# Expert rows gathered as two half rows from two tables instead of as whole rows from one, beside weight streaming with six raw buffers

## Chip, cores and metric

One core of a Trainium2 chip. The metric is device time in microseconds of one execution of the whole layer. The kernel before takes 2120.93 us, the median of 3 runs (2119.68 to 2122.23).

## What is computed

One encoder layer over 256 tokens of width 2048, all in float32. Two mixers and a cross attention come first. The last part, and the one that the change touches, is a feed-forward layer of 16384 single-neuron experts: for each token, 8 heads choose their 16 best experts each, and

```
u = u_tab[eb]
act = jax.nn.gelu(jnp.einsum('td,tkd->tk', xb, u))
out = jnp.einsum('tk,tkd->td', gb * act, v_tab[eb])
```

with `eb` the 128 chosen experts of a token and `gb` their softmax gates. `u_tab` and `v_tab` have 16384 rows of 2048 numbers (8 KB). The result is added to the tokens and normalized.

## The kernel before

The experts are split into two groups on the host. Three quarters (96 of 128 groups of 128 experts) are handled densely: all tokens times all of these experts, as matrix products on TensorE (PE), with the gates of experts that a token did not choose at zero. The other quarter (4096 experts, tables `Us` and `Vs`) is handled sparsely: for each token the rows of its chosen experts are gathered from memory.

Dense side. The products come in 12 chunks of 1024 experts. A weight tile of 128x1024 numbers, 512 KB, is loaded by SP's DMA queue into a raw buffer (`raw`), ACT rounds it to a high part (`hi`, line 1079), VectorE (DVE) subtracts to get the low part (`lo`, line 1085), and PE multiplies with both (lines 128 and 131 for `U`; 939 to 941 for `V`). The function `run` (line 1066) walks a list of such steps by hand-written lead times: `load(t + 8)`, `high(t + 3)`, `low(t + 2)`, then the products of step t. There are six raw buffers there (lines 1068 and 1069: four of the pool and two more), and the load into a buffer waits for DVE's `low` that read it last. A step may also be a load of gate values (`gd`), which DVE multiplies into the activations (line 1033). The list holds first steps of `V` and `U` chunks in turn, then steps of `V` alone.

Sparse side. `chosen` (line 1156) makes a list of tasks, each for one slot of all 128 tokens of a half: a `dot` (line 1139) on DVE multiplies the gathered `Us` rows with the tokens and sums, and an `axpy` (line 1147) on DVE adds the gathered `Vs` rows, scaled, to the result `hh`. After every step, `run` calls `wv.pump`, which hands DVE tasks in at a fixed rate. The gather of a task is issued three tasks ahead (`AHEAD = 3`) by `rows` (line 1119): one indirect DMA from POOL (GpSimd) that fetches 128 rows of 8 KB by an index per partition into one of four buffers `ring` in turn (`gat0`, `gat1`, `gat2` and `h1`, the last shown as `h`). An index that is out of bounds fetches nothing. Since a ring has four buffers, a gather waits until DVE is done with the task four before.

Spill. A token may have more chosen sparse experts than its 36 slots hold. `spill` (line 1191), which runs once late in the list of steps, takes up to 256 of these in two batches: `fetch` (line 1184) gathers their `Us` rows, their tokens from `hn`, and later their `Vs` rows, also by indirect DMAs from POOL. What is beyond that is left to `rest` (line 1213), behind a branch.

At the end `v_final` (line 1234) does the last chunk's products of `V` while DVE finishes the last axpys, and normalizes.

SP's queue loads raw tiles, and POOL's queue does the gathers; both kinds of DMA run on the same 16 DMA engines.

Of the kernel before, what the change touches and what calls it, by code (L numbers as in the profile page):

```python
# [20 lines left out]
T = 256  # L21
# [12 lines left out]
RD = 96  # L34
RS = P - RD
NS = RS * P
# [35 lines left out]
def hybrid_layer_kernel(ctx: ExitStack, tc: tile.TileContext, a: dict, out: bass.AP, dbg=None):  # L72
    nc = tc.nc
    V, A, G, PE = nc.vector, nc.scalar, nc.gpsimd, nc.tensor
# [21 lines left out]
    def slot(tag, shape, name, dt=F32):  # L96
        return b8.tile(shape, dt, tag=tag, name=name, bufs=3 if tag == "ms" else 2)
# [306 lines left out]
    for i in range(3):  # L404
        t = slot("qs" if i == 0 else "ms", [P, TT, 1024], "qkv"[i])
# [221 lines left out]
    hn = dp.tile([T, D], F32, name="hn")  # L627
# [53 lines left out]
    i1T, rT, gtT, key, work, gsp, sel, idx = ({} for _ in range(8))  # L681
# [384 lines left out]
    def run(steps):  # L1066
# [47 lines left out]
        for t in sorted(later):  # L1114
            for f in [x[0] for x in later[t]] + [x[1] for x in later[t]]:
                if f:
                    f()

    def rows(tab, tt, k):
        gat = ring[turn[0] % len(ring)]  # L1120
        turn[0] += 1
        G.indirect_dma_start(gat, None, a[tab], bass.IndirectOffsetOnAxis(ap=idx[tt][:, k:k + 1], axis=0),  # L1122
                             bounds_check=NS - 1, oob_is_err=False)
        return gat

    turn = [0]
# [29 lines left out]
    def chosen(blocks):  # L1156
        tasks = []
        for m in range(len(blocks) + 1):
            for k in range(8):
                if m < len(blocks) and k < blocks[m][2]:  # L1160
                    tasks.append((dot, "Us") + blocks[m] + (k,))
                if m > 0 and k < blocks[m - 1][2]:
                    tasks.append((axpy, "Vs") + blocks[m - 1] + (k,))
        held = []
        for m in range(len(tasks) + AHEAD):
            if m < len(tasks):
                f, tab, tt, k0, n, k = tasks[m]
                held.append(rows(tab, tt, k0 + k))
            if m >= AHEAD:
                f, tab, tt, k0, n, k = tasks[m - AHEAD]  # L1170
                if f is dot and k == 0:
                    weigh(tt, k0, n)
                    yield 0.225 * n
                if f is dot:
                    hold(tt)
                f(tt, k0, n, k, held[m - AHEAD])
                if f is dot and not any(t[0] is dot and t[2] == tt for t in tasks[m - AHEAD + 1:]):
                    hold(min([t[2] for t in tasks[m - AHEAD + 1:] if t[0] is dot], default=tt))
                yield 2.2
# [3 lines left out]

    def fetch(tab, ix, tag):
        t = tp.tile([P, D], F32, tag=tag, name="spl")
        src = hn if tab is None else a[tab]
        G.indirect_dma_start(t, None, src, bass.IndirectOffsetOnAxis(ap=ix, axis=0),
                             bounds_check=(T if tab is None else NS) - 1, oob_is_err=False)
        return t

    def spill():
        od = cp.tile([P, OV], F32, name="od")
        for b in range(OV):
            bs = slice(b, b + 1)
            u, x = fetch("Us", spl["i"][:, bs], "ah"), fetch(None, spl["ti"][:, bs], "al")
            yield
            yield
            V.scalar_tensor_tensor(u, u, 1.0, x, op0=ALU.mult, op1=ALU.mult, accum_out=od[:, bs])
            yield
        spl["v"] = [fetch("Vs", spl["i"][:, b:b + 1], ("ah", "al")[b]) for b in range(OV)]  # L1200
        A.activation(od, od, AF.Gelu_apprx_tanh)
        V.tensor_tensor(od, od, spl["g"], op=ALU.mult)
        spl["oh"] = rp.tile([P, OV, T], F32, tag="eq", name="oh")
        for b in range(OV):
            for tt in range(TT):
                bs = slice(b, b + 1)
                V.tensor_scalar(spl["oh"][:, b, tt * P:(tt + 1) * P], iota, spl["t"][:, bs], od[:, bs],
                                op0=ALU.is_equal, op1=ALU.mult)
                V.tensor_scalar(spl["t"][:, bs], spl["t"][:, bs], -float(P), None, op0=ALU.add)
        yield  # L1210
        done.add("spill")
# [140 lines left out]
def _wstat(w):  # L1352
    n = w.shape[1] // P
    return np.ascontiguousarray(w.reshape(2, 8, P, n, P).transpose(3, 0, 2, 1, 4)).reshape(n, 2, P, 1024)


def _xstat(w):
    n = w.shape[1] // 512
    return np.ascontiguousarray(w.reshape(8, 2, P, n, 512).transpose(3, 0, 2, 1, 4)).reshape(n, 8, P, 1024)


def _cols(v):
    return np.asarray(v).reshape(-1, P).T


def _actT(x):
    return np.ascontiguousarray(x.T.reshape(4, 4, P, T).transpose(0, 2, 1, 3)).reshape(4, P, 1024)


def _constants():  # L1370
    pos = np.arange(T, dtype=np.float32)
    inv = np.float32(10000.0) ** (-np.arange(64, dtype=np.float32) / np.float32(64))
    ang = (pos[:, None] * inv.astype(np.float32)[None, :]).astype(np.float32)
    cs = np.stack([np.cos(ang.astype(np.float64)), np.sin(ang.astype(np.float64))], axis=1)
    cs = cs.astype(np.float32).reshape(TT, P, 2, 64).transpose(1, 0, 2, 3)
    t = np.arange(T)
    lag = t[None, :] - t[:, None]
    same = (t[None, :] // 64) == (t[:, None] // 64)
    keep = (same | (lag > 0)).astype(np.float64)
    gam = 1.0 - 2.0 ** (-5.0 - np.arange(HD))  # L1380
    m = keep[None] * gam[:, None, None] ** np.abs(lag)[None] * 128.0 ** -0.5
    md = np.concatenate([m[:, :P, :], m[:, P:, P:]], axis=2).astype(np.float32)
    iota = np.tile(np.arange(P, dtype=np.float32), (P, 1))
    lane = np.arange(P)
    tri = np.concatenate([lane[:, None] < lane[None, :], lane[:, None]], axis=1).astype(np.float32)
    return {"cs": np.ascontiguousarray(cs), "md": np.ascontiguousarray(md), "iota": iota, "tri": tri,
            "ident": np.eye(P, dtype=np.float32)}


def arrange(i):  # L1390
    i = {k: np.asarray(v) for k, v in i.items()}
    w_in = i["w_in"][0]
    d = dict(_constants())
    d["x"] = i["x"][0].reshape(TT, P, D)
    d["mem"] = i["mem"][0].reshape(TT, P, D)
    d["xT"] = _actT(i["x"][0])
    d["memT"] = _actT(i["mem"][0])
    d["small"] = np.concatenate(
        [_cols(i["mix_norm_g"][0]), _cols(i["mem_norm_g"][0]), _cols(i["xattn_norm_g"][0]),
         _cols(i["ffn_norm_g"][0]), _cols(i["ret_gn_g"][0]),  # L1400
         i["conv_w"][0].reshape(4, 8, P).transpose(2, 1, 0).reshape(P, 32), _cols(i["conv_b"][0]),
         i["b_rg"][0].T, i["b_ig"][0].T, _cols(i["lru_lambda"][0]), _cols(i["lru_norm_g"][0])], axis=1)
    d["wri"] = np.stack([i["w_rg"][0], i["w_ig"][0]], axis=2)
    d["w_qkv"] = _xstat(w_in[:, :3072])
    d["w_xyg"] = _wstat(np.concatenate([w_in[:, 4096:], w_in[:, 3072:4096]], axis=1))
    d["w_out"] = _xstat(i["w_out"][0])
    d["w_xo"] = _xstat(i["w_xo"][0])
    d["w_xv"] = _xstat(i["w_xv"][0])
    d["w_xk"] = _wstat(i["w_xk"][0])
    d["w_xq"] = _wstat(i["w_xq"][0])  # L1410
    d["w_pq"] = _wstat(i["peer_w_q"][0])
    d["keysT"] = i["peer_sub_keys"][0].reshape(16, P, P).transpose(2, 0, 1)
    lane = np.arange(P)
    where = lane[None, :] * P + (lane[:, None] - lane[None, :]) % P
    u, v = i["peer_u"][0], i["peer_v"][0]
    d["U"] = u[where[:RD]].reshape(RD, P, 2, 8, P).transpose(0, 2, 4, 3, 1).reshape(RD, 2, P, 1024)
    d["V"] = v[where[:RD]].reshape(NCH, 4, 2, P, 4, 512).transpose(0, 4, 1, 3, 2, 5).reshape(NCH, 4, 4, P, 1024)
    d["Us"] = u[where[RD:].reshape(-1)]
    d["Vs"] = v[where[RD:].reshape(-1)]
    d["fng"] = i["ffn_norm_g"].reshape(1, D)  # L1420
    d["fg"] = i["final_norm_g"].reshape(1, D)
    return {k: np.ascontiguousarray(v) for k, v in d.items()}
# [16 lines left out]
```

## Time and profile before

| | before |
|---|---|
| median of 3 runs | 2120.93 us (2119.68 to 2122.23) |
| the profiled execution's own time | 2113.98 us |
| its span, first to last instruction | 2112.2 us |
| granted TensorE clock, mean | 0.989 |
| bytes moved by DMA | 542.91 MB |

The profile is of one execution. Its page gives busy times of the engines, the DMA queues (q1 is SP's, q0 is POOL's), the chain of waits that ended last and the costliest groups of instructions by line. The trace behind it is asked for busy time by stage, for who waited for whom, for the instructions of an engine in order of time, and for how long DMAs took from issue to landing. A row such as `L1122 POOL DMA_INDIRECT ... x69 | 118.3, 1714 | 688.9 <-...` reads: line 1122, POOL, 69 instructions, 118.3 us busy, 1714 ns mean, and 688.9 us of idle time before them with what ended it. [...]

### The profile page before, as it was taken

To read this page: it belongs to the slowest core of one execution; us is meant where nothing else is said; L and a number is where in the kernel's file an instruction comes from. 1 tells how busy PE (TensorE), PEld (TensorE's weight loads), DVE (VectorE), ACT (ScalarE), POOL (GpSimd) and SP (SyncE) were. 2 spreads that over 40 slices of the span, in tenths; PEclk is the share of its full clock that TensorE was granted. 3 is DMA by queue.
4 is the path that set the end of the run, shared out by engine and by line. 5 is a ranking of instruction groups with operands and counts; after the bars stand their busy time and mean duration, and the time that the engine had idled before them with its cause. 6 is when DMAs were issued, how large, how long until landed. Compare 5 with 4: busy or idle time off the path is not lost. (4 is left out here: it accounts for less than half of the span.)

```text
span 2112.2 us, 29016 instructions
## 1 busy us (share of the span) xinstructions
PE 2035.2 (96%) x10452; PEld 1729.0 (82%) x10452; DVE 1701.2 (81%) x2421; ACT 1038.6 (49%) x1592; POOL 375.9 (18%) x211
## 2 busy tenths in 40 slices
PE   8999998999999999999999979999999999999997
PEld 6877787888888888888889978888888888777776
DVE  6847967744554457999987769999999999999897
ACT  6565343444544355554578853544435444433334
POOL 0312221000000000000010002323233323453332
PEclk9999999999999999999999989999999999999999
DMA  8665555566654468555576569999999999999874
GB/s 279 237 220 159 170 192 170 158 192 195 188 177 144 131 188 281 177 173 181 187 269 206 171 229 342 380 378 398 368 365 335 348 377 415 375 411 402 298 265 152
DMA packets 155014, 542.91 MB, mean 257 GB/s; under 512 B 17136, under 2 KB 44400, under 8 KB 136560
## 3 DMA queue, kind: packets, MB, share of 16 engines
q1 hardware_dynamic: 132832, 400.48, 55.7%
q0 software_dynamic: 22032, 140.53, 16.7%
q8 instruction: 82, 1.34, 0.3%
q14 instruction: 68, 0.56, 0.1%
HBM read 541.99 MB, written 18.87 MB: 266 GB/s over the span
## 5 line engine op out<-in xcount | busy, mean ns | idle before, releaser
L120 DVE TENSOR_TENSOR lo<-raw,hi 128x1024 fp32r<-128x1024 f32 x396 | 499.5, 1277 | 242.4 <-PE xc L171 136.6
L119 ACT CAST hi<-raw 128x1024 fp32r<-128x1024 f32 x396 | 415.1, 1050 | 302.0 <-PE xc L172 164.7
L1079 ACT CAST hi<-raw 128x1024 fp32r<-128x1024 f32 x272 | 285.1, 1050 | 273.7 <-PE acc L941 143.2
L128 PE MATMUL U<-xn,hi 128*128 128x512 f32 x1536 | 381.4, 396 | 6.1 <-ACT hi L119 6.1
L1085 DVE TENSOR_TENSOR lo<-raw,hi 128x1024 fp32r<-128x1024 f32 x272 | 328.5, 1221 | 27.4 <-issue 17.6
L128 PEld LDWEIGHTS U<-xn,hi 128*128 128x128 f32 x1536 | 283.6, 190 | 59.9 <-ACT hi L119 6.2
L1122 POOL DMA_INDIRECT gat<-in_Us_dram,idx x69 | 118.3, 1714 | 688.9 <-DVE gat L1139 428.1
L131 PE MATMUL U<-xn,lo 128*128 128x256 f32 x1536 | 210.7, 286 | 7.7 <-DVE lo L1085 5.8
L131 PEld LDWEIGHTS U<-xn,lo 128*128 128x128 f32 x1536 | 200.5, 192 | 16.7 <-DVE lo L1085 6.8
L1139 DVE SCALAR_TENSOR_TENSOR gat<-gat,h 128x2048 f32<-128x2048 f32 x69 | 157.7, 2286 | 3.7 <-DMA gat<-in_Us_dram,idx 3.7
L940 PE MATMUL acc<-lo,ah 128*128 128x512 f32 x384 | 150.9, 393 | 5.7 <-DVE lo L1085 2.8
L939 PE MATMUL acc<-hi,ah 128*128 128x512 f32 x384 | 149.5, 392 | 1.6 <-DVE foldu L926 0.9
L941 PE MATMUL acc<-hi,al 128*128 128x512 f32 x384 | 150.3, 391 | 0.0
L128 PE MATMUL wb<-hT,hi 128*128 128x512 f32 x448 | 113.0, 396 | 0.0
L1122 POOL DMA_INDIRECT gat<-in_Vs_dram,idx x39 | 80.2, 2057 | 133.5 <-DVE hh L1147 111.5
L128 PEld LDWEIGHTS wb<-hT,hi 128*128 128x128 f32 x448 | 81.4, 189 | 14.8
L1147 DVE SCALAR_TENSOR_TENSOR hh<-gat,coef,hh 128x2048 f32<-128x2048 f32 x39 | 91.6, 2348 | 0.1
L940 PEld LDWEIGHTS acc<-lo,ah 128*128 128x128 f32 x384 | 72.4, 189 | 23.4 <-DVE lo L120 3.9
L128 PE MATMUL wb<-xT,hi 128*128 128x512 f32 x368 | 90.2, 397 | 0.2 <-ACT hi L119 0.2
L939 PEld LDWEIGHTS acc<-hi,ah 128*128 128x128 f32 x384 | 72.5, 189 | 17.7 <-DVE foldu L926 1.3
L940 PE MATMUL acc<-lo,xe 128*128 128x512 f32 x192 | 76.6, 399 | 8.7 <-DVE lo L1085 8.7
L941 PEld LDWEIGHTS acc<-hi,al 128*128 128x128 f32 x384 | 72.4, 189 | 14.9
(410 smaller groups left out, 3790.5 us busy)
## 6 DMA issues: line engine op xcount, KB each, us to landing
raw<-in_U_dram SPq DMA_DIRECT2D x192, 512.0 KB, 5.0
raw<-in_V_dram SPq DMA_DIRECT2D x192, 512.0 KB, 7.6
raw<-in_w_xyg_dram SPq DMA_DIRECT2D x48, 512.0 KB, 4.6
raw<-in_w_qkv_dram SPq DMA_DIRECT2D x48, 512.0 KB, 4.0
raw<-in_w_xk_dram SPq DMA_DIRECT2D x32, 512.0 KB, 3.6
raw<-in_w_xv_dram SPq DMA_DIRECT2D x32, 512.0 KB, 4.2
raw<-in_w_out_dram SPq DMA_DIRECT2D x32, 512.0 KB, 3.5
raw<-in_w_xq_dram SPq DMA_DIRECT2D x32, 512.0 KB, 3.5
```

Of the source, the lines that this page charges most:

```text
L119: A.copy(hi, raw)
L120: V.tensor_tensor(lo, raw, hi.bitcast(F32), op=ALU.subtract)
L128: PE.matmul(pt, hi[:, k * P:(k + 1) * P], xt[:, kb, :], start=(kb == 0), stop=(kb == KB - 1))
L131: PE.matmul(pt[:, :T], lo[:, k * P:(k + 1) * P], xt[:, kb, :T], start=False, stop=False)
L939: PE.matmul(pt, ah[:, c, t_], hi[:, w], start=(first and c == 0), stop=False)
L940: PE.matmul(pt, ah[:, c, t_], lo[:, w], start=False, stop=False)
L941: PE.matmul(pt, al[:, c, t_], hi[:, w], start=False, stop=(last and c == 7))
L1079: A.copy(his[t], raws[t])
L1085: V.tensor_tensor(los[t], raws[t], his[t].bitcast(F32), op=ALU.subtract)
L1122: G.indirect_dma_start(gat, None, a[tab], bass.IndirectOffsetOnAxis(ap=idx[tt][:, k:k + 1], axis=0), bounds_check=NS - 1, oob_is_err=False)
L1139: V.scalar_tensor_tensor(gat, gat, 1.0, h[0], op0=ALU.mult, op1=ALU.mult, accum_out=dots[tt, k0][:, k:k + 1])
L1147: V.scalar_tensor_tensor(hh[tt], gat, coef[tt, k0][:, k:k + 1], hh[tt], op0=ALU.mult, op1=ALU.add)
```

## The change

The host cuts `Us` and `Vs` into two tables each, `Us0`, `Us1`, `Vs0`, `Vs1`, of 4096 rows of 1024 numbers (4 KB). A new function `gather` issues two indirect DMAs with the same indices, into columns 0 to 1023 and 1024 to 2047 of the same buffer. `rows` calls it for every task, and `fetch` for the spill's rows of `Us` and `Vs`; the spill's tokens from `hn` are still fetched whole.

```diff
+    def gather(dst, tab, ix):
+        for n in range(2):
+            G.indirect_dma_start(dst[:, n * 1024:(n + 1) * 1024], None, a[f"{tab}{n}"],
+                                 bass.IndirectOffsetOnAxis(ap=ix, axis=0),
+                                 bounds_check=NS - 1, oob_is_err=False)
+
     def rows(tab, tt, k):
         gat = ring[turn[0] % len(ring)]
         turn[0] += 1
-        G.indirect_dma_start(gat, None, a[tab], bass.IndirectOffsetOnAxis(ap=idx[tt][:, k:k + 1], axis=0),
-                             bounds_check=NS - 1, oob_is_err=False)
+        gather(gat, tab, idx[tt][:, k:k + 1])
         return gat
...
     def fetch(tab, ix, tag):
         t = tp.tile([P, D], F32, tag=tag, name="spl")
-        src = hn if tab is None else a[tab]
-        G.indirect_dma_start(t, None, src, bass.IndirectOffsetOnAxis(ap=ix, axis=0),
-                             bounds_check=(T if tab is None else NS) - 1, oob_is_err=False)
+        if tab is None:
+            G.indirect_dma_start(t, None, hn, bass.IndirectOffsetOnAxis(ap=ix, axis=0),
+                                 bounds_check=T - 1, oob_is_err=False)
+        else:
+            gather(t, tab, ix)
         return t
...
-    d["Us"] = u[where[RD:].reshape(-1)]
-    d["Vs"] = v[where[RD:].reshape(-1)]
+    for n in range(2):
+        ns = slice(n * 1024, (n + 1) * 1024)
+        d[f"Us{n}"] = u[where[RD:].reshape(-1), ns]
+        d[f"Vs{n}"] = v[where[RD:].reshape(-1), ns]
```

On POOL, at the first step of the spill (`spl` are the spill's buffers, `gat0` to `gat2` and `h1` the ring), there stands before:

```order
L1122 DMA h1_4191<-in_Vs_dram,idx_10948 128x2048
L1187 DMA spl_16178<-in_Us_dram,spi_11079 128x2048
L1187 DMA spl_16182<-hn_6486,spti_11078 128x2048
L1122 DMA gat0_11272<-in_Us_dram,idx_10948 128x2048
L1122 DMA gat1_11273<-in_Vs_dram,idx_10948 128x2048
```

and now, at the same place:

```order
L1121 DMA h1_4191<-in_Vs0_dram,idx_10948 128x1024
L1121 DMA h1_4191<-in_Vs1_dram,idx_10948 128x1024
L1121 DMA spl_16502<-in_Us0_dram,spi_11079 128x1024
L1121 DMA spl_16502<-in_Us1_dram,spi_11079 128x1024
L1192 DMA spl_16509<-hn_6486,spti_11078 128x2048
L1121 DMA gat0_11272<-in_Us0_dram,idx_10948 128x1024
L1121 DMA gat0_11272<-in_Us1_dram,idx_10948 128x1024
L1121 DMA gat1_11273<-in_Vs0_dram,idx_10948 128x1024
L1121 DMA gat1_11273<-in_Vs1_dram,idx_10948 128x1024
```

Each expert gather has become two that follow each other directly, and `gat0` has two more DMAs ahead of its last one than before. The last four gathers of the sparse side, on POOL ahead of the branch of `rest`, before:

```order
L1122 DMA gat0_11272<-in_Vs_dram,idx_10948 128x2048
L1122 DMA gat1_11273<-in_Vs_dram,idx_10948 128x2048
L1122 DMA gat2_11274<-in_Vs_dram,idx_10948 128x2048
L1122 DMA h1_4191<-in_Vs_dram,idx_10948 128x2048
L1220 TENSOR_LOAD many_17526
```

and now:

```order
L1121 DMA gat0_11272<-in_Vs0_dram,idx_10948 128x1024
L1121 DMA gat0_11272<-in_Vs1_dram,idx_10948 128x1024
L1121 DMA gat1_11273<-in_Vs0_dram,idx_10948 128x1024
L1121 DMA gat1_11273<-in_Vs1_dram,idx_10948 128x1024
L1121 DMA gat2_11274<-in_Vs0_dram,idx_10948 128x1024
L1121 DMA gat2_11274<-in_Vs1_dram,idx_10948 128x1024
L1121 DMA h1_4191<-in_Vs0_dram,idx_10948 128x1024
L1121 DMA h1_4191<-in_Vs1_dram,idx_10948 128x1024
L1227 TENSOR_LOAD many_17970
```

There are eight in place of four, the two halves of a buffer side by side. On PE, DVE, ACT and SP every instruction stands where it stood.

## The prediction

> **What bounds the kernel now.** I read the page first, then the busy time by stage, then who waits for whom in the one stage where PE is not full, then the POOL timeline there. The page's shares, DMA packets and DMA queues:
>
> ```profile
> PE 2035.2 (96%) x10452; PEld 1729.0 (82%) x10452; DVE 1701.2 (81%) x2421; ACT 1038.6 (49%) x1592; POOL 375.9 (18%) x211
> DMA packets 155014, 542.91 MB, mean 257 GB/s; under 512 B 17136, under 2 KB 44400, under 8 KB 136560
> q1 hardware_dynamic: 132832, 400.48, 55.7%
> q0 software_dynamic: 22032, 140.53, 16.7%
> ```
>
> 155014 − 136560 = 18454 packets have 8 KB or more, and 144 gathers of 128 rows would make 18432 (fewer by rows whose index is out of bounds): a gathered row travels as one packet. So the change does what it says, 8 KB packets become pairs of 4 KB.
>
> Gathers run from about 1270 us on. The table by stage (length, then busy time of PE, PEld, DVE, ACT, POOL, granted clock, DMA share, GB/s):
>
> ```profile
> core 0: us, PE busy (x) PEld busy (x) DVE busy (x) ACT busy (x) POOL busy (x), PEclk, DMA share, GB/s
> 1270.00:1560.00 290.00, 285.38 (x1435) 243.03 (x1434) 276.62 (x282) 127.60 (x161) 91.19 (x53) 1.00 0.97 376
> 1560.00:1800.00 240.00, 238.87 (x1232) 204.98 (x1231) 233.31 (x239) 108.86 (x142) 78.64 (x45) 1.00 0.96 368
> 1800.00:1960.00 160.00, 146.35 (x620) 115.84 (x619) 154.94 (x154) 60.69 (x62) 74.05 (x32) 0.99 0.99 394
> 1960.00:2050.00 90.00, 90.00 (x370) 69.19 (x369) 79.40 (x71) 33.79 (x36) 27.02 (x16) 1.00 0.79 283
> 2050.00:2085.00 35.00, 31.60 (x129) 24.52 (x128) 32.82 (x24) 12.56 (x17) 13.88 (x7) 0.95 0.65 201
> ```
>
> PE is the bound up to 1800 and from 1960 to 2050. From 1800 to 1960 (products with V alone, and the spill) PE loses 160 − 146.35 = 13.65 us. Who was waited for there, DVE's one long wait, PE's two and ACT's longest:
>
> ```profile
> DVE gat L1139 <- DMA gat<-in_Us_dram,idx: 3.7, 1, 3.7
> ...
> DVE lo L1085 <- ACT hi L1079: 0.2, 1, 0.2
> PE acc L940 <- DVE lo L1085: 11.5, 11, 3.3
> PE V L940 <- DVE lo L1085: 2.1, 4, 0.8
> ACT hi L1079 <- DMA raw<-in_V_dram: 37.1, 19, 4.1
> ```
>
> PE waits for the `lo` pieces of DVE (11.5 + 2.1 = 13.6), and DVE is full: its only long wait is 3.7 us, once, for a gather. ACT waits 37.1 us for raw tiles, but DVE waits only 0.2 for ACT, so late raw tiles cost nothing now. In this stage DVE's order, with dots and axpys ahead of `lo`, is the bound, and what DVE waits for a gather goes straight to PE. In 2050 to 2085, the tail, DVE is full too (32.82 of 35).
>
> **The change part by part.** It touches POOL's queue alone; what the other engines execute, and in what order, is as before. Which gathers double, from the groups by line on POOL:
>
> ```profile
> L1122 POOL DMA_INDIRECT gat<-in_Us_dram,idx x69 | 118.3, 1714 | 688.9 <-DVE gat L1139 428.1 <-PE U L131 233.8 <-DVE hh L1147 9.8
> L1122 POOL DMA_INDIRECT gat<-in_Vs_dram,idx x39 | 80.2, 2057 | 133.5 <-DVE hh L1147 111.5 <-DVE gat L1139 19.4 <-DVE more L1217 1.7
> L1122 POOL DMA_INDIRECT h<-in_Vs_dram,idx x33 | 61.7, 1870 | 109.1 <-DVE hh L1147 102.0 <-DVE h L1139 6.8 <-DVE lo L1085 0.3
> L1122 POOL DMA_INDIRECT h<-in_Us_dram,idx x3 | 5.4, 1788 | 7.2 <-DVE h L1139 3.7 <-DVE hh L1147 3.2 <-ACT act L927 0.3
> ```
>
> 69 + 39 + 33 + 3 = 144 gathers and the spill's 4 expert gathers: 148 more POOL instructions. POOL's idle time in these rows is waiting for DVE to free a ring buffer, so POOL itself has room. The price of one more is seen where gathers stand back to back, at the first spill (POOL timeline, then three DVE rows of the same stretch):
>
> ```profile
> 1849.57 2.89 POOL L1187 DMA_INDIRECT spl<-in_Us_dram,spi  x1 [2.57 <-issue]
> 1852.76 7.62 POOL L1187 DMA_INDIRECT spl<-hn,spti  x1 [0.31 <-issue]
> 1860.68 1.72 POOL L1122 DMA_INDIRECT gat<-in_Us_dram,idx  x1 [0.30 <-issue]
> 1862.71 1.19 POOL L1122 DMA_INDIRECT gat<-in_Vs_dram,idx  x1 [0.30 <-issue]
> ...
> 1866.46 1.97 POOL L1122 DMA_INDIRECT h<-in_Vs_dram,idx  x1 [0.30 <-DVE lo L1085]
> 1861.81 1.23 DVE L1085 TENSOR_TENSOR lo<-raw,hi 128x1024 fp32r<-128x1024 f32 x1 [0.22 <-ACT hi L1079]
> 1862.95 2.35 DVE L1147 SCALAR_TENSOR_TENSOR hh<-h,coef,hh 128x2048 f32<-128x2048 f32 x1
> ...
> 1872.42 2.29 DVE L1139 SCALAR_TENSOR_TENSOR gat<-gat,h 128x2048 f32<-128x2048 f32 x1 [3.71 <-DMA gat<-in_Us_dram,idx]
> ```
>
> A gather behind another takes 0.30 us of gap and 1.72, 1.19 or 1.97: on average 1.9 us together, 1.5 at best and 7.9 at worst (the 7.62 row). I take 1.9. The 1862.71 gather ends at 1863.90, 0.95 us after DVE changed operations at 1862.95, so it seems to be let in between two DVE operations; that is why a full DVE makes the price uncertain. From 1800 to 1960 POOL goes from 74.05 us to 74.05 + 30 × 1.63 = 123 of 160 (30 of its 32 instructions are split): not a bound, but each gather is complete later. Issue to landing of the gathers from 1270 to 1800, from 1800 to 1960 and in the tail:
>
> ```profile
> DMA to landing us min/median/max: 7.0/9.4/11.3
> DMA to landing us min/median/max: 7.9/11.1/17.2
> DMA to landing us min/median/max: 5.1/6.4/6.9
> ```
>
> Cover: four ring buffers, and a gather is issued 0.3 us after DVE frees its buffer. 144 uses in some 800 us are 5.6 us apart, so the data are wanted 4 × 5.6 − 2.35 (the use itself) = 20 us after that: with 9.4 to land, about 10 us to spare. A second half 1.9 us later is hidden there. From 1270 to 1800 I price the split at 0.5 us, between 0 and 5 (should some second halves need the 7.9).
>
> Where gathers queue up, their rate counts too. The gathers issued at 1860.68, 1862.71 and 1866.46 landed after
>
> ```profile
> DMA to landing us min/median/max: 11.7/11.7/11.7
> DMA to landing us min/median/max: 13.5/13.5/13.5
> DMA to landing us min/median/max: 17.2/17.2/17.2
> ```
>
> that is at 1872.38, 1876.21 and 1883.66: with the one between them, 3.76 us for each 1.05 MB, or 279 of the stage's 394 GB/s, 0.71. That is what one 8 KB packet to one 4 KB packet of the raw queue gives (two thirds). With 4 KB packets on both sides it is half, 197 GB/s or 5.3 us a gather: up to 1.5 us more for each one queued. [...]
>
> [...]
>
> First spill: the gather issued at 1860.68 had DVE waiting already. Ahead of its last byte now stand two more second halves on POOL (the spill's `Us` and its own): 2 × 1.9 = 3.8; its last transfer is half a gather, 5.3 / 2 in place of 3.76: −1.1; the queue before it at half share: 0 to 1.5, say 0.8. Sum 3.5 us, all of it DVE waiting and so PE (0 to 8). The later spill steps and the 11.1 us landings elsewhere in 1800 to 1960 have more room: 1 us each, 0 to 4 each.
>
> Tail: DVE does an axpy and a `lo` every 3.4 us, and each gather waits for an axpy. One of the last four, its use, and its landing:
>
> ```profile
> 2053.18 2.98 POOL L1122 DMA_INDIRECT gat<-in_Vs_dram,idx  x1 [1.67 <-DVE more L1217]
> 2062.23 2.34 DVE L1147 SCALAR_TENSOR_TENSOR hh<-gat,coef,hh 128x2048 f32<-128x2048 f32 x1
> DMA to landing us min/median/max: 6.8/6.8/6.8
> ```
>
> It landed at 2059.98 and was used at 2062.23: 2.25 us to spare. A pair on POOL takes 2.98 + 1.9 = 4.9, more than the 3.4 us pace, so the last four fall back 1.5 us each after the first: 1.9 − 1.0 (half a transfer) + 3 × 1.5 − 2.25 = 3.2, call it 3, between 0 and 6. The `lo` pieces stand behind these axpys, and PE waits for them.
>
> Nothing is credited: DVE's time is what it was.
>
> Sum: 0.5 + 3.5 + 1 + 1 + 3 = 9.0 us, on the profiled execution's 2113.98: 2123.0. That execution lies 6.95 us below the median of the three runs, 2120.93; the same 9 us on the median give 2129.9, say **2130**.
>
> **The rivals.** (1) No change: the slack holds everywhere, 0 to 4 us, 2121. For it: one wait for a gather in the whole kernel. Against: the zero slack at 1872 and 2.25 in the tail.
>
> (2) Faster: the raw tiles, now on one third of the DMA engines while gathers queue, get half. ACT's 37.1 us of waits go, `lo` follows, PE's 13.6 us go: 2120.93 − 13.6 = 2107. It decides if DVE's `lo` is late because of its inputs; the point is that DVE would have to be idle 10 us and more from 1800 to 1960, and it waits 3.7 + 0.2.
>
> (3) Much slower: the DMA engines are the bound. By the queue rows a packet of q1 takes 0.557 × 2112.2 × 16 / 132832 = 142 ns at 3.0 KB, one of q0 256 ns at 6.4 KB: 34 ns a KB and 39 ns of each packet. 128 more packets of a gather on 16 engines are 0.31 us. From 1800 to 1960, 30 of them, 9 us at a share of 0.99; from 1270 to 1800, 96 of them, 30 us where some 3.5% of 530, 18 us, are free: 12. With the tail's 3: 2121 + 24 = 2145. Against it: two queues of mixed packet size make the 39 ns doubtful, and raw tiles have cover.
>
> **How the numbers follow.** A measurement here can tell about 0.2%, 4.2 us. The late gathers 0.52, no change 0.22, faster 0.12, much slower 0.14: slower 0.66, same 0.22, faster 0.12. The likeliest case alone spans 2122 to 2142 (its terms' lower and upper ends, not all at once). The range, 2117 to 2146, leaves out the faster case and the upper part of the third rival.
>
> **What would show it.** Right: 148 more POOL instructions of about 1.6 us; landings of the pairs 1 to 3 us longer than 9.4 and 11.1; DVE waiting for gathers some 8 to 12 us in place of 3.7, at the first spill and in the tail; ACT's waits for raw tiles below 37.1 and PE none the better for it. Wrong: PE's 13.6 us from 1800 to 1960 shrinking (the second rival), DMA share at 1.0 with raw tiles later throughout (the third), or DVE waits for gathers before 1800.

## The result and the profile after

The changed kernel takes 2130.91 us, the median of 6 runs (2129.45 to 2134.82); the kernel before, on the same chip, 2119.92 us (6 runs, 2116.93 to 2122.23). The ratio is 1.0057, 95% interval 1.0047 to 1.0068: slower by some 12 us (10 to 14; the two medians are 11.0 apart). The profiled execution took 2129.58 us, its span 2127.8 us, granted clock 0.984.

The page of the changed kernel: engines, DMA packets, and POOL's queue.

```profile
PE 2041.0 (96%) x10452; PEld 1734.7 (82%) x10452; DVE 1697.0 (80%) x2421; ACT 1039.3 (49%) x1592; POOL 648.6 (30%) x359
DMA packets 176329, 542.96 MB, mean 255 GB/s; under 512 B 21936, under 2 KB 49200, under 8 KB 174384
q0 software_dynamic: 43344, 140.55, 17.3%
```

POOL has 359 − 211 = 148 instructions more and 272.7 us more of busy time, 1.84 us each. Packets of 8 KB or more fell from 18454 to 1945, so the rows do travel in halves. But the DMA engines' time for q0 rose only from 16.7% to 17.3%, with twice the packets (43344 for 22032): a packet has no large fixed price here, some 12 ns for each further one.

POOL's gathers by line:

```profile
L1121 POOL DMA_INDIRECT gat<-in_Us_dram,idx x138 | 266.4, 1931 | 576.3 <-DVE gat L1144 301.0 <-PE U L131 232.5 <-issue 22.9
L1121 POOL DMA_INDIRECT gat<-in_Vs_dram,idx x78 | 153.0, 1962 | 62.4 <-DVE hh L1152 39.5 <-issue 15.2 <-DVE gat L1144 4.4
L1121 POOL DMA_INDIRECT h<-in_Vs_dram,idx x66 | 109.3, 1656 | 46.9 <-DVE hh L1152 28.4 <-issue 11.6 <-DVE h L1144 3.2
```

One instruction costs what it cost before (1.66 to 1.96 us against 1.71 to 2.06). What shrank is POOL's idle time in front of them: for rows of `Vs` it was 133.5 and 109.1 us, now 62.4 and 46.9.

The table by stage (columns as before: length, busy PE, PEld, DVE, ACT, POOL, granted clock, DMA share, GB/s), for the same stretches:

```profile
1270.00:1560.00 290.00, 285.40 (x1435) 243.05 (x1434) 276.62 (x280) 127.28 (x161) 173.39 (x104) 1.00 0.98 375
1560.00:1800.00 240.00, 238.88 (x1232) 204.94 (x1231) 233.39 (x237) 108.55 (x141) 157.87 (x88) 1.00 0.97 365
1800.00:1960.00 160.00, 144.76 (x605) 115.25 (x604) 149.31 (x154) 60.33 (x62) 127.79 (x60) 0.97 1.00 383
1960.00:2050.00 90.00, 87.53 (x350) 66.57 (x350) 77.89 (x70) 31.16 (x32) 60.36 (x28) 0.98 0.84 287
2050.00:2085.00 35.00, 27.72 (x113) 21.62 (x111) 29.50 (x20) 9.75 (x10) 26.79 (x13) 0.90 0.64 198
```

Up to 1800 us nothing is lost, to a few hundredths of a microsecond, though POOL is twice as busy. All of the loss is behind 1800. DVE's waits for gathers in the whole sparse part (total, times, longest), which were 3.7 us in one wait:

```profile
DVE gat L1144 <- DMA gat<-in_Us_dram,idx: 7.2, 3, 3.3
DVE hh L1152 <- DMA gat<-in_Vs_dram,idx: 4.2, 2, 3.0
DVE hh L1152 <- DMA h<-in_Vs_dram,idx: 2.5, 2, 2.3
```

13.9 us, 10.2 us more: 8.3 of it from 1800 to 1960 us, the rest in the tail. What this does to PE, from 1800 us to the end, before and then after:

```profile
1800.00:2112.00 312.00, 285.71 (x1191) 223.58 (x1189) 282.05 (x276) 118.55 (x133) 119.21 (x56) 0.98 0.84 316
```

```profile
1800.00:2128.00 328.00, 291.41 (x1195) 228.94 (x1193) 283.70 (x281) 119.32 (x134) 225.11 (x106) 0.95 0.84 304
```

PE's idle time there goes from 26.3 to 36.6 us (+10.3, as much as DVE's new waits), and its busy time rises by 5.7 us for the same products, at a granted clock of 0.95 instead of 0.98. The sum, 16.0, is within 0.4 us the difference between the two profiled executions (2129.58 − 2113.98 = 15.6). That pair lies further apart than the medians, so a part of it belongs to these two executions and not to the change.

Where do the late gathers come from? POOL's order of time ahead of the spill (start, duration, line, operation, idle before it), and DVE's in the same stretch:

```profile
1809.11 1.73 POOL L1121 DMA_INDIRECT gat<-in_Us_dram,idx  x1 [7.13 <-DVE gat L1144]
1811.15 8.49 POOL L1121 DMA_INDIRECT gat<-in_Us_dram,idx  x1 [0.30 <-issue]
...
1834.71 7.57 POOL L1121 DMA_INDIRECT gat<-in_Us_dram,idx  x1 [0.30 <-issue]
...
1849.70 0.99 POOL L1121 DMA_INDIRECT gat<-in_Us_dram,idx  x1 [0.30 <-issue]
```

```profile
1806.51 2.32 DVE L1144 SCALAR_TENSOR_TENSOR gat<-gat,h 128x2048 f32<-128x2048 f32 x1
...
1812.11 2.39 DVE L1085 TENSOR_TENSOR lo<-raw,hi 128x1024 fp32r<-128x1024 f32 x2
...
1816.45 2.32 DVE L1144 SCALAR_TENSOR_TENSOR gat<-gat,h 128x2048 f32<-128x2048 f32 x1
1818.66 0.12 DVE L1144 DVE_READ_ACCUMULATOR gat<-gat,h 128x1 f32 x1
...
1841.33 0.09 DVE L1144 DVE_READ_ACCUMULATOR gat<-gat,h 128x1 f32 x1
...
1843.60 2.35 DVE L1152 SCALAR_TENSOR_TENSOR hh<-h,coef,hh 128x2048 f32<-128x2048 f32 x1
1845.86 2.51 DVE L1085 TENSOR_TENSOR lo<-raw,hi 128x1024 fp32r<-128x1024 f32 x2
1851.66 2.29 DVE L1144 SCALAR_TENSOR_TENSOR gat<-gat,h 128x2048 f32<-128x2048 f32 x1 [3.29 <-DMA gat<-in_Us_dram,idx]
```

Two POOL instructions took 8.49 and 7.57 us in place of 1.9. While DVE runs operation after operation without a pause they don't finish; they end 0.98 and 0.95 us after the start of the short row in which DVE reads out its accumulator behind a dot (1811.15 + 8.49 = 1819.64 against 1818.66; 1842.28 against 1841.33). By these rows POOL is shut out until DVE passes such a point, and then needs about 0.95 us. In the last row DVE stands waiting, and the same instruction takes 0.99 us. From 1809 to 1878 POOL is back to back (0.30 us between instructions), and at 1851.66 DVE waits for the first time. The kernel before has such long instructions too: 5 of its 150 indirect DMAs take over 4 us, against 10 of 298 now. All five of before, and seven of the ten now, end 0.93 to 0.98 us behind the start of a read-out, and one more 0.87 us after DVE began to wait; what let in the other two is not to be seen.

### The profile page after: what moved, and what is told of

It is laid out like the page before. It is cut to its first block, busy times and chain, and to the rows that moved or that the text cites. A ratio compares the mean times of both kernels' runs of the same rounds, so it can differ in the third digit from the quotient of the medians.

```text
span 2127.8 us, 29431 instructions
## 1 busy us (share of the span) xinstructions
PE 2041.0 (96%) x10452; PEld 1734.7 (82%) x10452; DVE 1697.0 (80%) x2421; ACT 1039.3 (49%) x1592; POOL 648.6 (30%) x359
## 3 DMA queue, kind: packets, MB, share of 16 engines
q0 software_dynamic: 43344, 140.55, 17.3%
## 4 chain that ended last, share of the span: by engine, by line
PE 76%; DVE 14%; DMA 4%; issue 2%; POOL 2%; ACT 2%; DVEq 0%; POOLq 0%; ACTq 0%; SPq 0%
PE U L128 14%; PE U L131 7%; PE wb L128 6%; PE xc L171 6%; PE xc L172 6%; PE xc L170 6%; PE acc L940 5%; PE acc L941 5%; PE acc L939 5%; DVE lo L120 4%; PE wb L131 3%; PE G L873 2%; PE V L940 2%; PE V L941 2%; PE V L939 2%
## 5 line engine op out<-in xcount | busy, mean ns | idle before, releaser
L1121 POOL DMA_INDIRECT gat<-in_Us_dram,idx x138 | 266.4, 1931 | 576.3 <-DVE gat L1144 301.0
L131 PEld LDWEIGHTS U<-xn,lo 128*128 128x128 f32 x1536 | 200.2, 191 | 16.7 <-DVE lo L1085 6.7
L1121 POOL DMA_INDIRECT gat<-in_Vs_dram,idx x78 | 153.0, 1962 | 62.4 <-DVE hh L1152 39.5
L1121 POOL DMA_INDIRECT h<-in_Vs_dram,idx x66 | 109.3, 1656 | 46.9 <-DVE hh L1152 28.4
L940 PE MATMUL acc<-lo,xe 128*128 128x512 f32 x192 | 77.7, 405 | 14.1 <-DVE lo L1085 14.1
```

Of the source, the lines that this page charges most:

```text
L131: PE.matmul(pt[:, :T], lo[:, k * P:(k + 1) * P], xt[:, kb, :T], start=False, stop=False)
L940: PE.matmul(pt, ah[:, c, t_], lo[:, w], start=False, stop=False)
L1121: G.indirect_dma_start(dst[:, n * 1024:(n + 1) * 1024], None, a[f"{tab}{n}"], bass.IndirectOffsetOnAxis(ap=ix, axis=0), bounds_check=NS - ...
```

## The experiments

Theory: each gather's second POOL instruction makes it late, above all where DVE shuts POOL out. Rivals: the 4 KB packets lose against the raw tiles in the queues; the DMA engines pay for each packet; the shut-outs alone, or the number of instructions alone, are the cost. Every run below is compared with the kernel before on the same chip; "over" means over it.

### More instructions without the packets

`tiny_twin`, whole gathers with a useless small one ahead of each:

```diff
+        G.indirect_dma_start(tiny[turn[0] % 4], None, a[tab + "t"], <same indices>)
         G.indirect_dma_start(gat, None, a[tab], <indices>)
```

> Every gather of expert rows is whole again (one 8 KB piece per row, as before the change), but each is preceded by a gather of the first 64 bytes of the same 128 rows into a spare tile that nobody reads, the spill's two gathers of expert rows too: GpSimd has as many instructions as after the change (148 more than before), the big transfers travel as before. Theory 1, the second GpSimd instruction makes gathers late (1.9 us each, now and then 5 to 8.5): about as slow as the change, 8 to 11 us over the kernel before, VectorE's waits for gathers 10 to 16 us instead of 3.7, again just before the spill and in the tail. Theory 2, the 4 KB pieces lose against the raw transfers in the queues: as the kernel before, 0 to 2 us over it, waits for gathers 3 to 6 us. Theory 3, the DMA engines are bound by the number of pieces: the small pieces are as many as the change added, so also 8 to 11 us, but then with the DMA engines' time of GpSimd's queue well above the 16.7% of before.

Measured: ratio 1.0078 (1.0057 to 1.0098), 16.5 us over. DVE's waits for gathers:

```profile
DVE gat L1142 <- DMA gat<-in_Us_dram,idx: 14.2, 2, 8.5
DVE hh L1150 <- DMA h<-in_Vs_dram,idx: 6.5, 1, 6.5
DVE hh L1150 <- DMA gat<-in_Vs_dram,idx: 5.0, 1, 5.0
```

25.7 us with the big rows in 8 KB packets as before, and q0's share of the DMA engines at 16.9%. The half packets are not needed for the loss, so the second theory falls, and with q0's time at that of before the third does too. (The small rows travel several to a packet: q0 has 4736 packets more than before, not 21312 as with the halves. I had expected as many pieces; the loss comes without them.) Here the cost is even above the forecast of 8 to 11.

`tiny_behind`, the same with the two lines the other way round:

> As tiny_twin (whole gathers, and as many GpSimd instructions as the change has, by a gather of 64 bytes per row that nobody reads), but the small gather stands behind the big one instead of ahead of it. A gather's own transfer then starts as early as before the change if GpSimd is free; only the gathers after it are pushed back. If what costs is a gather's own second instruction (its data complete about 2 us later, and more where that instruction is shut out): 0 to 3 us over the kernel before. If it is GpSimd's queue as a whole, back to back from 1809 us to 1878 us in the changed kernel and held up there by instructions of 5 to 8.5 us: 7 to 14 us over it, with waits for gathers before the spill and in the tail as in tiny_twin.

Measured: 1.0076 (1.0051 to 1.0100), 16.1 us over, waits 19.1 us in three (8.6, 5.5, 5.0). A gather's own second instruction isn't what costs, since here it stands behind; it is POOL's queue as a whole. Why a useless small gather costs a little more than a second half is not settled; the two intervals overlap with the change's.

### Where it costs

Four mixes of whole gathers (`whole`: one indirect DMA from a table of whole rows, kept beside the halves) and half gathers, by the number of the gather. The spill's fetches of expert rows are whole in `halves_early` and, as the only ones, in `halves_but_spill`:

```diff
-        gather(gat, tab, idx[tt][:, k:k + 1])
+        gather(gat, tab, idx[tt][:, k:k + 1], whole=turn[0] > 100)    # halves_early
+        gather(gat, tab, idx[tt][:, k:k + 1], whole=turn[0] <= 100)   # halves_late
+        gather(gat, tab, idx[tt][:, k:k + 1], whole=turn[0] > 131)    # halves_but_tail
```

> Half gathers for the first 100 gathers (used up to about 1810 us), whole gathers for the last 44 and for the spill. Theory 1 (late gathers cost only where there is no slack, from 1800 us on): as the kernel before, 0 to 2 us over it. Theory 2 or 3 (a toll on every half gather): about 100 of 148 shares of the 11.0 us, 6 to 8 us over it.

> Whole gathers for the first 100, half gathers for the last 44 and for the spill. Theory 1: as the changed kernel, 9 to 12 us over the kernel before, with VectorE's waits for gathers about 14 us. A toll on every half gather: 3 to 5 us over it.

> Half gathers except for the last 13, which are used in the tail from about 2060 us. Theory 1: the tail's 5.5 us of VectorE waits go, the 8.3 us of 1800 to 1960 stay: 4 to 7 us over the kernel before. If the tail's waits only stand for lateness that was carried into it from earlier: 9 to 11 us over it, with the tail's waits still there.

> Half gathers everywhere but in the spill, whose four fetches of expert rows are whole again (4 GpSimd instructions fewer than the changed kernel, all between 1850 and 1880 us). The prediction laid 3.5 us on the first spill and 1 us on the later ones: by that, 5 to 8 us over the kernel before. By the trace of the changed kernel the lateness there comes from two shut-out instructions ahead of the spill (8.49 us at 1811 and 7.57 us at 1835): 9 to 12 us over it, as the changed kernel.

Measured: `halves_early` 1.0001 (0.9989 to 1.0013); `halves_late` 1.0044 (1.0031 to 1.0057), 9.3 us over, waits 12.2 us; `halves_but_tail` 1.0014 (1.0002 to 1.0025), 3.0 us over, with no wait for a gather behind 2050; `halves_but_spill` 1.0034 (1.0022 to 1.0047), 7.2 us over.

100 pairs of halves in the first part cost nothing, 44 pairs at the end nearly all: no toll by the piece. The tail and the spill each carry a part: whole gathers in the tail take away 9 us of the change's 12 (the forecast said 5 to 8), and four whole fetches in the spill some 5 (2 to 8). Together that is more than there is, so the parts aren't independent. Of the last expectation the prediction's reading holds (5 to 8 us): by the trace alone I had put the lateness at the spill on the two instructions ahead of it, but the spill's own instructions count as well.

One trace is one execution, and here executions differ much. The traced one of `halves_but_tail` is the longest of its twelve (2130.51 us, the shortest is 2116.22), and DVE waits 16.2 us for gathers in it, all ahead of 2050 us, more than in the changed kernel's trace. The traced one of `halves_but_spill` is the longest of its six (2137.05 us, waits 17.0), that of `halves_late` the shortest of its five (2123.95). So the shares of tail and spill rest on the medians, and how often a long instruction comes is in part chance. The longest POOL instruction of all the traces is in `halves_but_tail`; DVE reads out its accumulator twice while it runs, at 1924.33 and 1927.67 us, without letting it end:

```profile
1915.61 15.31 POOL L1125 DMA_INDIRECT gat<-in_Us_dram,idx  x1 [0.30 <-issue]
```

### Opening POOL's door

If POOL gets in behind a read-out, one more read-out per pair of gathers should help. `door_after` is the changed kernel with an output on each axpy that nobody reads:

```diff
-        V.scalar_tensor_tensor(hh[tt], gat, coef[tt, k0][:, k:k + 1], hh[tt], op0=ALU.mult, op1=ALU.add)
+        V.scalar_tensor_tensor(hh[tt], gat, coef[tt, k0][:, k:k + 1], hh[tt], op0=ALU.mult, op1=ALU.add,
+                               accum_out=junk[:, 0:1])
```

> The changed kernel, with an accumulated output (written to a spare column that nobody reads) on every scaled addition of a V row, so that VectorE reads its accumulator out behind it, as it does behind every dot. In the traces so far GpSimd's long instructions ended 0.95 us behind such a read-out, so this opens a second door for them per pair of gathers. Shut-out theory: instructions over 4 us fall from 10 to 4 or fewer, VectorE's waits for gathers from 13.9 us to 4 to 9, the time by 3 to 8 us against the changed kernel, to 3 to 8 us over the kernel before; the added read-outs (72 of 0.08 us) cost under 2 us. Count theory (1.9 us for each instruction, wherever it falls; the long ones are chance): as the changed kernel, 10 to 13 us over the kernel before.

Measured: 1.0009 (0.9996 to 1.0023), 1.9 us over: some 10 us (6.6 to 13.8) of the change's 12 are gone, with all 148 further instructions and all half packets in place. POOL's groups and DVE's waits in `door_after`:

```profile
L1121 POOL DMA_INDIRECT gat<-in_Us_dram,idx x138 | 234.3, 1698 | 593.4 <-DVE gat L1144 316.4 <-PE U L131 234.6 <-issue 23.2
L1121 POOL DMA_INDIRECT gat<-in_Vs_dram,idx x78 | 141.4, 1812 | 66.6 <-DVE hh L1152 42.7 <-issue 14.0 <-DVE gat L1144 5.9
```

```profile
DVE gat L1144 <- DMA gat<-in_Us_dram,idx: 3.3, 1, 3.3
DVE hh L1152 <- DMA gat<-in_Vs_dram,idx: 1.0, 2, 0.6
DVE hh L1152 <- DMA h<-in_Vs_dram,idx: 1.0, 1, 1.0
```

The mean fell little (1.93 to 1.70 us, 1.96 to 1.81), but only one instruction of over 4 us is left of ten, and the waits went from 13.9 to 5.3 us. What the mean lost is nearly all in the long ones: nine of them less, at some 5 us above the usual 1.9 each, make the 43 us by which the time of POOL's indirect DMAs fell. So the long instructions make the loss. And up to 1845 us, where POOL was back to back in the changed kernel, it waits for DVE again and again (at the spill behind it, it is back to back here too); about 1840 us, in order of time:

```profile
1840.74 1.97 POOL L1121 DMA_INDIRECT gat<-in_Vs_dram,idx  x1 [0.30 <-issue]
1844.32 1.74 POOL L1121 DMA_INDIRECT gat<-in_Us_dram,idx  x1 [1.62 <-DVE gat L1144]
```

The pair is done at 1842.71 us, before the next buffer is free: POOL waits 1.62 us for DVE again.

`doors_after` and `doors_before` add read-outs to the `lo` subtractions as well:

```diff
-                    V.tensor_tensor(los[t], raws[t], his[t].bitcast(F32), op=ALU.subtract)
+                    V.scalar_tensor_tensor(los[t], raws[t], 1.0, his[t].bitcast(F32), op0=ALU.mult,
+                                           op1=ALU.subtract, accum_out=junk[:, 1:2])
```

> As door_after, and the subtractions that make the low halves of the weights from 1220 us on have an accumulated output as well (the same subtraction, written as a scaled one), so that nearly every VectorE operation there is followed by a read-out. Shut-out theory: no GpSimd gather over 4 us, most near 1 to 2 us, waits for gathers 1 to 5 us; the 360 or so added read-outs of 0.08 us cost 0 to 10 us where VectorE is full (160 us of 1800 to 1960 hold about 90 of them, 7 us at most if none is hidden): minus 8 to plus 5 us against the changed kernel. Count theory: waits for gathers stay at 12 to 16 us, and the time is that of the changed kernel or above.

> The kernel before the change (whole gathers) with the same read-outs as in doors_after. Shut-out theory: GpSimd's gathers fall from 1.71 to 2.06 us towards 1.0 to 1.5, the instructions over 4 us from 5 to none, VectorE's waits for gathers from 3.7 us to under 2; the time changes by minus 3 to plus 5 us, as the read-outs' own cost decides. Count theory: no change in GpSimd's durations, 0 to 5 us slower.

Measured: 1.0044 (1.0028 to 1.0059) and 1.0049 (1.0030 to 1.0068), 9.3 and 10.4 us over. With doors everywhere half gathers cost no more than whole ones, as far as these two intervals can tell (to some 5 us; waits 1.1 and 0 us). Two details were missed: one instruction of over 4 us is left in `doors_after` (5.09 us), and the means in `doors_before` are 1.70 to 1.75 us, where 1.0 to 1.5 was expected. And the added read-outs themselves cost 10 us, twice the most that I expected of `doors_before`; the subtraction takes 1.22 us in either form, so its new form isn't the cost. Their row in it:

```profile
L1085 DVE DVE_READ_ACCUMULATOR lo<-raw,hi 128x1 f32 x272 | 22.7, 83 | 0.0
```

272 of 83 ns are 22.7 us, behind pieces that PE waits for; just under half of it shows. Where a read-out stands behind an axpy, which nobody waits for at once, 72 of them cost little: `door_before` is as fast as the kernel before, though a small cost may be set off there by the waits for gathers that are gone.

`door_before` is the kernel before with the read-outs on the axpys:

> The kernel before the change (whole gathers) with the read-out behind every scaled addition of a V row, as in door_after. Shut-out theory: its 5 GpSimd instructions of over 4 us fall to 0 or 1, VectorE's 3.7 us of waits for gathers to under 1.5; since 3.7 us is all that gathers cost here, 0 to 4 us below the kernel before, and below door_after by 1 to 5 us. If a read-out costs something by itself (as the 272 behind the subtractions do, doors_before being 10 us over), 0 to 3 us above it.

Measured: 1.0000 (0.9989 to 1.0012). DVE waits for no gather any more, and the gathers take POOL 1.70 to 1.85 us on the mean (1.71 to 2.06 before), the longest behind 1330 us under 4 us, but the hoped-for gain isn't there. No version here beats the kernel before.

### Shutting POOL's door

`no_door_before` and `no_door_after` take the read-out behind the dots away:

```diff
             dots[tt, k0] = tp.tile([P, 8], F32, tag="dots", name="dots", bufs=2)
+            V.memset(dots[tt, k0], 0.0)
-        V.scalar_tensor_tensor(gat, gat, 1.0, h[0], op0=ALU.mult, op1=ALU.mult,
-                               accum_out=dots[tt, k0][:, k:k + 1])
+        V.scalar_tensor_tensor(gat, gat, 1.0, h[0], op0=ALU.mult, op1=ALU.mult)
```

> The kernel before the change (whole gathers) without the accumulated output of the dots, so that no read-out follows them; the sums of the dots are left out (a zeroed tile stands in their place), all else runs. Shut-out theory: GpSimd has lost its surest door, its gathers take 2.5 to 5 us on the mean instead of 1.71 to 2.06, many of them over 4 us, VectorE waits 15 us or more for gathers, and the kernel is 8 us or more over the kernel before with half the GpSimd instructions of the change. Count theory: GpSimd's durations stay, VectorE's waits stay at 2 to 6 us, and the time is that of the kernel before or 0 to 5 us under it.

Measured: 1.0000 (0.9984 to 1.0016). The durations rise, though over the whole kernel only to means of 2.13 to 2.69 us (2.5 to 5 was expected); the loss of 8 us or more isn't there. POOL from 1800 to 1960 us, where the means are 3.0 to 4.1 us, and its longest instruction:

```profile
L1122 POOL DMA_INDIRECT gat<-in_Us_dram,idx x13 | 39.0, 3004 | 32.0 <-DVE gat L1140 24.8 <-DMA gat<-in_Vs_dram,idx 5.4 <-issue 1.8
L1122 POOL DMA_INDIRECT gat<-in_Vs_dram,idx x6 | 24.9, 4142 | 19.3 <-DVE hh L1147 19.0 <-issue 0.3
L1122 POOL DMA_INDIRECT h<-in_Vs_dram,idx x7 | 23.5, 3363 | 10.4 <-DVE hh L1147 9.8 <-issue 0.6
```

```profile
1854.24 10.78 POOL L1122 DMA_INDIRECT gat<-in_Us_dram,idx  x1 [0.30 <-issue]
```

13 instructions take over 4 us (5 in the kernel before), up to 10.78 us, and DVE doesn't wait once for a gather. So shut-outs alone aren't the cost either. (The 72 missing read-outs may hide up to 72 × 10.4 / 272 = 2.8 us of it.) The theory had to become a product: a shut-out costs time only where a second instruction per gather leaves POOL no time to make it good. The test is the same edit on the changed kernel:

> The changed kernel (half gathers) without the accumulated output of the dots, as in no_door_before; the sums of the dots are left out (a zeroed tile stands in their place). In no_door_before 26 gathers and 6 fetches of 1800 to 1960 us took GpSimd 94.14 us, 2.94 us each, and it cost no time, since one instruction per gather leaves GpSimd 66 us idle there. Product theory (a shut-out costs time only where a second instruction per gather leaves no idle time to make it good): 56 instructions of 2.94 and 0.30 us are 181 us where 160 are to be had, so GpSimd becomes the bound and the kernel is 15 to 40 us over the kernel before, with VectorE waiting 20 to 45 us for gathers. Count theory (only the 148 further instructions cost, 1.9 us each): as the changed kernel, 7 to 13 us over the kernel before. Shut-outs alone: as no_door_before, 0 to 3 us.

Measured: 1.0091 (1.0065 to 1.0117), 19.3 us over, in the range of the product theory and of no other. 26 instructions take over 4 us, where the changed kernel has 10. DVE's waits for gathers are 38.1 us, in an execution of 2147.88 us (the median is 2140.42):

```profile
DVE gat L1145 <- DMA gat<-in_Us_dram,idx: 21.4, 3, 10.5
DVE hh L1152 <- DMA h<-in_Vs_dram,idx: 13.9, 5, 7.1
DVE hh L1152 <- DMA gat<-in_Vs_dram,idx: 2.8, 2, 1.9
```

POOL didn't become a full bound (133.84 us of the 160, not 181). While DVE waits, POOL's instructions are short: in `tiny_twin`, where DVE waits 8.46 us for a gather up to 1880.95 us, the six that start from 1873.66 us on take 0.99 to 1.00 us each. That the same kept the 181 from coming here is an estimate.

The six kernels side by side, as us over the kernel before:

| | read-outs behind dots and axpys | behind dots | none |
|---|---|---|---|
| whole gathers | 0.0 | (the kernel before) | 0.0 |
| half gathers | 1.9 | 12.1 | 19.3 |

The size fits a simple account, an estimate from the rows above. In the changed kernel DVE takes a gather every 5.3 us there (the uses at 1806.51 and 1843.60 are seven apart). A pair takes POOL 2 × (0.30 + 1.9) = 4.4 us, so it catches up 0.9 us per gather; a single one takes 2.2 and catches up 3.1. A shut-out that adds 6 us is made good after two gathers when they are whole, and after six or seven when they are halved, and then the next one is there, 24 us on.

## Why the prediction came out

**The sum**, 9 us on the median, 2130, against 2130.91 measured, and its likeliest case, late gathers behind 1800 us, came true. The change itself is larger than the sum, 11 to 12 us on one chip; the total came so near in part because the median it was added to, 2120.93 of three runs, is 1 us above that of the six. POOL's 148 instructions at "about 1.6 us" measured 1.84. From the first half's issue to the second half's landing the pairs took 11.6 us up to 1800 us, 12.1 up to 1960 and 7.6 in the tail (medians), 2.2, 1.0 and 1.2 more than whole gathers: in or at the forecast 1 to 3. DVE's waits, "some 8 to 12 us in place of 3.7", measured 13.9.

**Mid stage, 0.5 us.** Right: `halves_early` shows none, and PE's busy time up to 1800 us is the same.

**First spill 3.5 and the rest to 1960 us, 2 us.** Right in size: waits of 8.3 for 3.7 us there, and `halves_but_spill` gives 5 (2 to 8) to the spill's own instructions. The reason given, the 1.9 us of each further second half, was half of it: the 7.6 us row that I had called the worst price, and then left out of the sum, is the kind that carries the loss, by coming again before POOL has made up for it. With the long ones gone (`door_after`) the same instructions cost 1.9 us (−0.8 to 4.9).

**Tail 3 us (0 to 6).** Too small: 5.5 us of waits in the profile, and 9 us less when its gathers are whole. The long instruction ahead of it was not thought of: one of 8.73 us starts at 2029.37 us.

**Queue rate, up to 1.5 us per gather.** Seen where gathers queue up, but it decided nothing. Before, from 1872.4 to 1883.7 us, 442 packets of q0 went beside 443 of q1, with 66.6% and 34.9% of the engines; now, from 1876.4 to 1891.7 us, 919 went beside 842, with 52.4% and 50.2%, and four gathers behind each other landed 5.1 us apart in place of 3.76. Over the whole stage, 1800 to 1960 us, the gathers' share did not fall, and the raw tiles won nothing. Before, and then after:

```profile
q1 hardware_dynamic: 8597, 31.38, 50.5%
q0 software_dynamic: 4608, 31.59, 48.7%
```

```profile
q0 software_dynamic: 8580, 30.88, 50.6%
q1 hardware_dynamic: 8262, 30.20, 48.7%
```

The step that failed is that this rate would decide anything: it held for a few gathers in a row after the spill. `tiny_twin`, without any 4 KB pieces of gathered rows, loses as much (16.5 us over).

**Rivals.** Faster: ACT's waits for raw tiles from 1800 to 1960 us went from 37.1 to 33.8 and PE's for `lo` in the `acc` products from 11.5 to 14.1, as the prediction said of its own case.

```profile
ACT hi L1079 <- DMA raw<-in_V_dram: 33.8, 18, 4.1
PE acc L940 <- DVE lo L1085: 14.1, 10, 5.0
```

Much slower by the packets' 39 ns: 21312 more packets on q0 raise its share of the 16 engines from 16.7% to 17.3%. That is some 250 us of engine time, or 12 ns for each, a third of the 39 ns.

**What was missed altogether** is the clock: 5.7 of the 15.6 us between the profiled executions are PE's busy time, the same products at a lower granted clock (the last section). That the sum, without this term, came within 1 us of the median owes something to chance: the tail was too small, this term was missing, and the typical execution loses less than the profiled pair shows.

## What to carry to other kernels

Before a DMA issued by POOL is cut in two, ask how much of the interval between two uses POOL has left afterwards, not whether it is busy: here 3.1 us per gather carried shut-outs of up to 10.78 us, and 0.9 us didn't. Where POOL issues indirect DMAs beside a DVE that never pauses, look at the longest POOL instructions and at what DVE did when each ended; the mean tells little (1.93 us with the loss, 1.70 without it). An accumulator read-out on a DVE operation that no one waits for was a cheap pause here (72 of them in `door_before`: 1.0000), though not one that always lets POOL in (the row of 15.31 us ran on past two); on one that PE waits for, 272 of them cost 10 us.

## What the runs showed of the hardware

POOL's instruction for a gather of 128 rows took 0.99 us when nothing was in its way (at 1849.70 us in the changed kernel, while DVE waited), and up to 10.78 us (`no_door_before`), in one case 15.31 (`halves_but_tail`), beside a row of two-input float32 operations of DVE. It got in at some boundaries between them and not at others: in the changed kernel the one at 1847.12 us, beside two `lo` subtractions, took 0.99 us too, and the one at 1811.15 us saw five operations pass. When a read-out came it nearly always got in: in the traces of the two kernels 45 of these instructions (7 and 38) ended 0.85 to 1.05 us behind the start of a read-out that came while they ran, and none ran on past one; in the twelve traces that have read-outs behind dots, some 630 ended so, and seven ran on past one. What decides it at the other boundaries is open. The rows above show the gathers held up with `lo` subtractions, dots and axpys over them. That POOL waits out one whole DVE instruction would not make 8 us: the dots and axpys take 2.3, and here five operations in a row passed. What of a gather is held up was not tried.

The granted clock fell behind two stalls of PE in the changed kernel, to 0.83 and 0.69 over the next 10 us. The two stalls, of 2.49 and 5.03 us, and the stretches of 10 us around the ends of both:

```profile
1810.03 0.50 PE L940 MATMUL acc<-lo,ah 128*128 128x512 f32 x1 [2.49 <-DVE lo L1085]
1860.65 0.79 PE L940 MATMUL acc<-lo,xe 128*128 128x512 f32 x1 [5.03 <-DVE lo L1085]
```

```profile
1800.00:1810.00 10.00, 7.54 (x34) 5.89 (x32) 9.75 (x24) 4.14 (x6) 2.57 (x3) 1.00 1.02 408
1810.00:1820.00 10.00, 9.97 (x37) 7.86 (x37) 10.00 (x8) 3.25 (x4) 9.39 (x3) 0.83 0.97 358
1820.00:1830.00 10.00, 10.00 (x45) 8.30 (x45) 10.00 (x9) 6.03 (x6) 8.88 (x4) 1.00 0.93 331
1860.00:1870.00 10.00, 9.35 (x30) 7.50 (x31) 10.00 (x8) 2.10 (x2) 8.78 (x5) 0.69 1.02 412
1870.00:1880.00 10.00, 10.00 (x46) 8.29 (x45) 7.49 (x8) 5.15 (x6) 7.17 (x6) 1.00 1.03 410
```

The 10 us behind the first run at 0.83 and behind the second at 0.69, then at 1.00 again: by this estimate the two stalls cost PE their own length and 1.7 or 3.1 us on top (10 × 0.17, 10 × 0.31). Not every short stall does so: in the kernel before, the first of the two is there as well, 2.45 us long up to 1809.06 us, and the 10 us from 1810 us stay at 1.00. That the stalls are the cause was not tried by itself, and why the same short one has a dip in one trace and none in the other is open.
